# Last ConvFFN of a hybrid backbone: down projection with tokens on partitions, accumulated in four PSUM banks while the features come

## The chip, the cores and the metric

One Trainium2 chip (trn2); the kernel runs on 1 core. The metric is device time in microseconds (us), of one launch. Engines: PE (matrix products; PEld is its loading of stationary operands), DVE, ACT, POOL, and SP, which issues most transfers.

## The reference

The trunk has two layers (DEPTH 2), on 256 context and 256 latent tokens of 1024 features. After the mixing sub-layer each layer has a ConvFFN; the last one runs on the latent tokens alone, and the result is normalised:

```python
def conv_ffn(h, w_up, cw, cb, w_down):
    u = depthwise_conv(h @ w_up, cw, cb, FFN_CONV // 2)
    up, gate = jnp.split(u, 2, axis=-1)
    return (jax.nn.gelu(gate) * up) @ w_down
...
        x = x + mx[5] * conv_ffn(modulate(rms_norm(x, norm_ffn[l]), mx[3], mx[4]),
                                 w_up[l], ffn_conv_w[l], ffn_conv_b[l], w_down[l])
...
    return rms_norm(x, final_norm)
```

`w_up` is 1024 x 5632, `w_down` 2816 x 1024, `mx[5]` a gate per feature, `rms_norm` divides a token by the root of its mean square over the 1024 features and multiplies by a gain per feature. All in float32.

## The kernel before

Activations are kept with features on partitions: `xr[j]` (j = 0 to 7) holds 128 features of all 512 tokens. Each float32 operand of a large product is split into two float32r tiles, high and low (`split`, L155: ACT casts the high part, L151; DVE subtracts for the low one, L158), and `gemm` (L137) issues three products per 128 features of the contraction: high x high, high x low, low x high. The helper `mm` records them all at L129.

Weights come in chunks of up to 1 MB (`chunk`, L161; three slots `raw`, issued by SP in program order), and are split in units of up to 128x1024 into three slots `wh` and three `wl` (`unit`, L192). A slot is free again when PE has done the products of the unit in it.

`ffn` (L1101) works on 22 tiles of 128 gated features, in pairs. For a pair it projects two `up` and two `gate` tiles (`project`, tile `proj`, 24 products of 256 columns each in the last layer), and for each `conv` (L1112) empties the PSUM bank in three passes: ACT's scaled copy (L1114) and two DVE passes for the neighbouring tokens (L1116, L1119). Then gelu (ACT, L1180), the product with `up` (POOL, L1181), and the split into the pair `gTh`, `gTl`. The projections rotate through five PSUM banks `mm`.

`down(k0, k1)` runs twice. After 16 feature tiles it takes the first 14: for each of 8 tiles of 128 output features `m`, the products with `w_down` (stationary) over 14 feature tiles (moving, 256 tokens) into one bank `down`, which DVE then adds into `xr[m]` with the gate (`residual`, L1066). After the last feature it takes the other 8 feature tiles, again for 8 tiles `m` (`finish`, L1077, tile `out`). There, behind each `m`, stand the addition into `xr[m]` (L1070), the square for the norm (ACT, L440, summed by POOL, L442), and `to_tokens` (L1194): DVE multiplies by the final gain (`yf`, L1198), PE transposes two blocks of 128x128 (`yt`, L1201), DVE and ACT copy them into the rows `y`. After the last one come the sums of squares over partitions (products with ones, tile `ss`), root, reciprocal, a scaling of four half rows `y` of 128x512 (L1295 on ACT, L1297 on DVE) and four stores (L1298).

At the start of the stage stand the sums of squares of the mixing sub-layer's result (`ss`), `1/rms` spread over the partitions by PE (`nb`), and `modulate` (L471) for 8 tiles: DVE `hf`, ACT `hh`, DVE `hl`. The first two `up` tiles are projected together, as the tiles `hh`, `hl` come.

The instructions are recorded in program order and a scheduler places them on each engine's queue, which then runs strictly in that order; `prio(150)` lets it take a part 150 instructions earlier.

```python
                    if together - 1 <= m < HELD[l]:
                        finish(
                            held, gT[k0:k1], [Y], gate, t0, squares, to_tokens if last else None,
                            cut=k1 - k0 - 2 if len(held) > 1 else 0,
                        )
```

Of the kernel before, what the change touches and what calls it, by code (L numbers as in the profile page):

```python
# [69 lines left out]
def backbone(ctx: ExitStack, tc: tile.TileContext, a: dict, out: bass.AP):  # L70
# [33 lines left out]
    def banks(alias={}, **tags):  # L104
        """A pool of PSUM banks under the given tags for a part of the program."""
# [12 lines left out]
    def prio(n):  # L118
        """The scheduler takes this part of the program so many instructions earlier."""
# [11 lines left out]
    def keep_busy(n, tag):  # L131
        """Products that nothing reads, to keep the array's clock up through a wait."""
# [11 lines left out]
    def warm(func):  # L144
        """Has the tables of func loaded ahead of its first use."""
# [9 lines left out]
    def split(hi, lo, src, lo_eng=None, hi_eng=None):  # L155
        """src = hi + lo exactly, each in float32r"""
# [41 lines left out]
    def columns(w, c0, c1):  # L198
        """Units of 128 columns of the weight matrix w (K <= 1024 rows), in order."""
# [7 lines left out]
    def run(main, side=None, every=1):  # L207
        """Emits a step of side, then so many steps of main, and so on to the end of both."""
# [58 lines left out]
    def params(l, eng, tag="raw", w=2048):  # L267
# [47 lines left out]
        # the queries come scaled for the softmax  # L315
# [3 lines left out]
        # softplus(-lam) = max(-lam, 0) + log1p(exp(-|lam|)), the second as 2 atanh(e / (2 + e))  # L319
# [53 lines left out]
    def ada_quarter(l, blk, part, col, res, tag):  # L373
        """A quarter of each of the two chunks."""
# [21 lines left out]
    def spread(steps, rate):  # L396
        """Emits rate of steps with each load of weights."""
# [15 lines left out]
    def gains(scale, g, fs=(slice(0, 8),), t=None):  # L413
        """norm gain times (1 + scale), per stream"""
# [8 lines left out]
    class SumSquares:  # L423
        """Sums squares of tiles of features, for n tokens, as the tiles come; the last ones stay apart
        and may come in ranges of tokens."""
# [4 lines left out]
        def add(self, i, t, eng=nc.gpsimd, r=None):  # L430
            """tile i"""
# [12 lines left out]
        def inv_rms(self, width, r=None, ps=None):  # L444
            """Token-major for tokens r: token r.start + 128 t + p at [p, t]."""
# [25 lines left out]
    def modulate(j, h, r, rb, gain, shift):  # L471
        """x / rms * gain + shift for tile j and the tokens r of a stream"""
# [9 lines left out]
    def modulated(hs, squares, t0, scale, col, shift, norm="norm_ffn"):  # L482
        """A function to call as the sums of a stream are there: for the FFN it emits the stream, else both at the last."""
# [32 lines left out]
    def project(u, xs, r, parts=None, tag="mm"):  # L516
        """[P features, tokens r of xs] of one unit of weights, in parts of the tokens"""
# [807 lines left out]
```

## Time and profile before

| | |
|---|---|
| time, median of 3 runs (all) | 1419.99 us (1418.11, 1419.99, 1420.43) |
| profiled execution: span from first to last instruction | 1416.0 us; its own time is not listed apart from these runs |
| mean granted TensorE clock | 0.988 |
| PE busy | 1374.2 us, 97% |
| PEld busy | 1172.5 us, 83% |
| DVE busy | 892.9 us, 63% |
| ACT busy | 668.8 us, 47% |
| POOL busy | 231.9 us, 16% |
| HBM | 193.02 MB read, 137 GB/s over the span |

How to read it: busy times are shares of the whole span, over stages with different limits. Products on PE are pipelined, so the duration of one (0.28 us for 256 columns) is longer than the distance to the next; the price of a product is the time of a gapless run divided by its count. Rows of the chain of waits give such runs. The last ConvFFN runs from about 1206 us to the end.

### The profile page before, as it was taken

The page shows a single profiled execution, that of the slowest core. Times are in us where ns is not written, and L with a number is a line of the kernel's source. Part 1 is how long each engine was busy: PE and PEld are TensorE (multiplying, and loading weights), DVE is VectorE, ACT ScalarE, POOL GpSimd, SP SyncE. Part 2 cuts the span into 40 slices and gives each one's busy share as a digit, 9 for nine tenths or more (in the row PEclk, how much of TensorE's full clock was granted, in tenths as well). Part 3 has the DMA queues.
Part 4 walks back from the last instruction along what each step waited for, and adds up shares of the span by engine and source line. Part 5 has one row for each costly group of instructions (what it writes and reads, how often), then busy time and mean ns, then how long its engine had stood idle before and what let it go on. Part 6 is the DMA issues. An engine that isn't in the chain of part 4 may idle for free.

```text
span 1416.0 us, 20938 instructions
## 1 busy us (share of the span) xinstructions
PE 1374.2 (97%) x8362; PEld 1172.5 (83%) x8362; DVE 892.9 (63%) x1451; ACT 668.8 (47%) x1136; POOL 231.9 (16%) x223
## 2 busy tenths in 40 slices
PE   7999999999999999999999999999999999999997
PEld 5676598888888898888888887878688899999997
DVE  3687648667634565555443543687788986777575
ACT  5575635423532444344322433475355665566454
POOL 2021013113200101211100111010122431122012
PEclk9999999999999999999999999999999999999999
DMA  9433715233233502222343337225465666455643
GB/s 332 135 107 131 272 35 170 80 97 100 79 100 110 172 31 90 86 96 87 89 123 120 104 116 245 62 80 191 152 219 183 197 190 199 135 194 175 196 140 100
DMA packets 187777, 195.41 MB, mean 138 GB/s; under 512 B 9340, under 2 KB 178290, under 8 KB 182560
## 3 DMA queue, kind: packets, MB, share of 16 engines
q1 hardware_dynamic: 186624, 193.23, 42.6%
q8 instruction: 65, 1.06, 0.3%
q0 software_dynamic: 1056, 0.86, 0.2%
q14 instruction: 32, 0.26, 0.1%
HBM read 193.02 MB, written 1.05 MB: 137 GB/s over the span
## 4 chain that ended last, share of the span: by engine, by line
PE 85%; DVE 7%; DMA 3%; ACT 2%; issue 2%; SPq 0%; POOL 0%; ACTq 0%; DVEq 0%; POOLq 0%
PE proj L129 49%; PE down L129 8%; PE out L129 7%; PE lat L129 4%; PE pa L129 3%; PE uf L129 2%; PE sc L129 2%; PE pv L129 2%; PE gt L129 2%; DVE wl L158 2%; PE pt L832 1%; DVE wh L153 1%; DMA raw<-in_w_in_dram 1%; DMA raw<-in_w_ada_dram 1%; PE kn L129 1%
## 5 line engine op out<-in xcount | busy, mean ns | idle before, releaser
L158 DVE TENSOR_TENSOR wl<-raw,wh 128x1024 fp32r<-128x1024 f32 (+9 forms) x339 | 339.4, 1014 | 160.8 <-ACT wh L151 156.1
L129 PE MATMUL proj<-hh,wh 128*128 128x512 f32 (+1 forms) x1232 | 417.8, 340 | 5.5 <-DVE sg L989 2.2
L129 PE MATMUL proj<-hh,wl 128*128 128x512 f32 (+1 forms) x1232 | 416.9, 339 | 0.2 <-DVE wl L158 0.2
L129 PE MATMUL proj<-hl,wh 128*128 128x512 f32 (+1 forms) x1232 | 416.8, 339 | 0.0
L151 ACT CAST wh<-raw 128x1024 fp32r<-128x1024 f32 (+7 forms) x275 | 216.3, 808 | 264.0 <-PE proj L129 153.9
L129 PEld LDWEIGHTS proj<-hh,wh 128*128 128x128 f32 x1232 | 236.1, 192 | 31.9 <-issue 3.1
L129 PEld LDWEIGHTS proj<-hh,wl 128*128 128x128 f32 x1232 | 236.1, 192 | 25.3 <-DVE wl L158 0.7
L129 PEld LDWEIGHTS proj<-hl,wh 128*128 128x128 f32 x1232 | 236.0, 192 | 24.5
L1181 POOL TENSOR_TENSOR gate<-gate,up 128x512 f32<-128x512 f32 (+1 forms) x44 | 55.3, 1257 | 445.4 <-ACT gate L1180 424.7
L153 DVE CAST wh<-raw 128x1024 fp32r<-128x1024 f32 x64 | 54.4, 853 | 52.7 <-PE proj L129 46.4
L129 PE MATMUL down<-gTh,wh 128*128 128x512 f32 (+1 forms) x224 | 75.5, 337 | 0.0
L129 PE MATMUL down<-gTh,wl 128*128 128x512 f32 (+1 forms) x224 | 75.4, 337 | 0.0
L129 PE MATMUL down<-gTl,wh 128*128 128x512 f32 (+1 forms) x224 | 75.3, 336 | 0.0
L158 DVE TENSOR_TENSOR gTl<-gate,gTh 128x512 fp32r<-128x512 f32 (+1 forms) x44 | 24.6, 559 | 78.5 <-ACT gTh L151 78.5
L129 PE MATMUL pa<-raw,cvec 128*32 128x512 f32 (+1 forms) x576 | 62.7, 457 | 3.9 <-DMA raw<-in_w_ada_dram 3.8
L442 POOL TENSOR_TENSOR sq<-sq,sq 128x256 f32<-128x256 f32 (+1 forms) x28 | 31.6, 1129 | 198.6 <-ACT sq L440 197.0
L1070 DVE SCALAR_TENSOR_TENSOR xr<-out,ada,xr 128x256 f32<-128x256 f32 x48 | 22.2, 480 | 44.1 <-PE out L129 44.1
L129 PE MATMUL out<-mh,wl 128*128 128x256 f32 (+1 forms) x152 | 47.4, 312 | 0.0
L129 PE MATMUL out<-mh,wh 128*128 128x256 f32 (+1 forms) x152 | 47.4, 313 | 0.0
L129 PE MATMUL out<-ml,wh 128*128 128x256 f32 (+1 forms) x152 | 47.4, 312 | 0.0
L151 ACT CAST gTh<-gate 128x512 fp32r<-128x512 f32 (+1 forms) x44 | 22.6, 514 | 51.3 <-POOL gate L1181 51.3
L129 PEld LDWEIGHTS down<-gTh,wh 128*128 128x128 f32 x224 | 42.5, 190 | 4.4
(287 smaller groups left out, 2725.3 us busy)
## 6 DMA issues: line engine op xcount, KB each, us to landing
raw<-in_w_up_dram SPq DMA_DIRECT2D x44, 1024.0 KB, 5.0
raw<-in_w_ada_dram SPq DMA_DIRECT2D x40, 1024.0 KB, 4.9
raw<-in_w_in_dram SPq DMA_DIRECT2D x30, 1024.0 KB, 5.3
raw<-in_w_down_dram SPq DMA_DIRECT2D x16, 896.0 KB, 5.2
raw<-in_w_ada_dram SPq DMA_DIRECT2D x32, 256.0 KB, 7.5
raw<-in_w_in_dram SPq DMA_DIRECT2D x16, 512.0 KB, 4.9
raw<-in_w_out_dram SPq DMA_DIRECT2D x8, 1024.0 KB, 5.3
raw<-in_w_down_dram SPq DMA_DIRECT2D x16, 512.0 KB, 3.8
```

What stands on the lines that cost most here:

```text
L129: pinned(nc.tensor.matmul(o, lhsT, rhs, start=start, stop=stop))
L151: nc.scalar.copy(out, in_)
L153: eng.tensor_copy(out, in_)
L158: (lo_eng or nc.vector).tensor_tensor(lo, src, hi, op=ALU.subtract)
L442: eng.tensor_tensor(self.terms[0][:, r], self.terms[0][:, r], sq[:, r], op=ALU.add)
L832: nc.tensor.transpose(o[:, c], probs[i][:, kt * P : (kt + 1) * P], ident)
L1070: nc.vector.scalar_tensor_tensor(xr[m][:, r], o[:, y], gate[:, s, m : m + 1], xr[m][:, r], op0=ALU.mult, op1=ALU.add)
L1181: nc.gpsimd.tensor_tensor(g, g, us[z], op=ALU.mult)
```

## The change

The code before the last ConvFFN stays. In the last layer `ffn` takes another path:

- `down` with tokens on partitions: for a feature tile `k`, the features `gT[k]` (128 features x 128 tokens) are the stationary operand and a row block of `w_down` (128 features x 512 output features) the moving one. Four sums (2 token tiles x 2 halves of the output features) stay in four PSUM banks `acc` over all 22 feature tiles. The products of the pair `i - 2` follow the projections of the pair `i`.
- the projections have three banks `mm`; the first two use banks `acc`, which are not needed yet.
- `row_of` spreads the gate of the output features over all partitions (8 products with the identity, two copies by ACT), and the final gain is loaded as such rows by a transfer that POOL issues.
- `token_major` transposes the residual to tokens, in two steps inside the stage (16 blocks of 128x128, four copies of 128x512 by ACT).
- `down_last` takes the last four feature tiles: 18 and 19 for all four banks, then 20 and 21 bank by bank. Behind each bank: times the gate row, plus the residual (DVE, 128x512), square with its sum over the row (ACT), times the gain (POOL, for the last bank DVE). Behind each token tile: root, reciprocal, scaling of two half rows (DVE and ACT), two stores.
- `to_tokens`, `final_gains` and the sums of squares over partitions go.

```diff
-    def finish(held, xs, qs, gate, t0, squares, also=None, then=None, cut=0):
+    def finish(held, xs, qs, gate, t0, squares, then=None, cut=0):
...
+        accs, rows_ = [], {}
+        def row_of(cols):
+            t = slot("row", "row", F32, D)
+            for z in range(2):
+                o = bank("rowb", "mm")
+                for i in range(4):
+                    j = 4 * z + i
+                    mm(o[:, i * P : (i + 1) * P], cols[:, j : j + 1].to_broadcast([P, P]), ident, True, True)
+                nc.scalar.copy(t[:, z * 512 : (z + 1) * 512], o)
+            return t
+        def token_major():
+            rows_["gain"] = slot("row", "row", F32, D)
+            nc.gpsimd.dma_start(rows_["gain"], a["final_norm"].unsqueeze(0).to_broadcast([P, D]))
+            rows_["gate"] = row_of(ada_cols[2][:, 1, 8:16])
+            yield
+            rows_["x"] = [slot("xt", "row", F32, D) for _ in range(2)]
+            for tt in range(2):
+                for z in range(2):
+                    o = bank("xtb", "mm")
+                    for i in range(4):
+                        nc.tensor.transpose(
+                            o[:, i * P : (i + 1) * P], xr[4 * z + i][:, CTX + tt * P : CTX + (tt + 1) * P], ident
+                        )
+                    nc.scalar.copy(rows_["x"][tt][:, z * 512 : (z + 1) * 512], o)
+                yield
+        def down_part(k, w, tt, z):
+            if not accs:
+                accs.extend([bank("acc") for _ in range(2)] for _ in range(2))
+            q, c = slice(tt * P, (tt + 1) * P), slice(z * 512, (z + 1) * 512)
+            gemm(accs[tt][z], [(gT[k][0][:, q], gT[k][1][:, q], w[0][:, c], w[1][:, c])], k == 0, k == NF - 1)
+        def down_tokens(k):
+            ws = down_weights(k)
+            for i in range(2):
+                for tt in range(2):
+                    for z in range(2):
+                        down_part(k + i, ws[i], tt, z)
+        def down_last(k):
+            ws = {}
+            for k2 in range(k, NF, 2):
+                ws[k2], ws[k2 + 1] = down_weights(k2, "wd")
...
+            for tt in range(2):
+                for z in range(2):
+                    for k2 in range(first, NF):
+                        down_part(k2, ws[k2], tt, z)
+                    with prio(150):
+                        c, y = slice(z * 512, (z + 1) * 512), ys[tt][z]
+                        nc.vector.tensor_tensor(y, accs[tt][z], rows_["gate"][:, c], op=ALU.mult)
+                        nc.vector.tensor_tensor(y, y, rows_["x"][tt][:, c], op=ALU.add)
+                        junk = slot("sq", "s", F32)
+                        nc.scalar.activation(junk, y, AF.Square, accum_out=ssq[:, tt, z : z + 1])
+                        e = nc.vector if tt and z else nc.gpsimd
+                        e.tensor_tensor(yg[tt][z], y, rows_["gain"][:, c], op=ALU.mult)
+                with prio(150):
+                    r = small.tile([P, 1], F32, tag="ry", name=nm("ry"), bufs=2)
+                    nc.vector.tensor_tensor(r, ssq[:, tt, 0:1], ssq[:, tt, 1:2], op=ALU.add)
+                    nc.scalar.activation(r, r, AF.Sqrt, bias=eps, scale=1.0 / D)
+                    nc.vector.reciprocal(r, r)
+                    nc.vector.tensor_scalar(yg[tt][0], yg[tt][0], r, None, op0=ALU.mult)
+                    nc.scalar.activation(yg[tt][1], yg[tt][1], AF.Copy, scale=r)
+                    for z in range(2):
+                        nc.sync.dma_start(out[0, tt * P : (tt + 1) * P, z * 512 : (z + 1) * 512], yg[tt][z])
...
+        if last:
+            side = token_major()
+            with phase("ffn", gT=16, c=8, row=4, wd=8, y=8):
+                with banks(acc=4, mm=3):
+                    next(side)
+                    for i in range(0, NF, 2):
+                        pair_of_tiles(i)
+                        if 2 <= i < NF - 2:
+                            down_tokens(i - 2)
+                        if i >= 4:
+                            next(side, None)
+                    down_last(NF - 4)
+            return
...
-    squares = SumSquares(8, T - CTX)
-    ffn(1, columns_of[1], adas[1], True, h_ffn1, ups1, None, squares, None, None)
-    r = squares.inv_rms(D)
...
+    ffn(1, columns_of[1], adas[1], True, h_ffn1, ups1, None, None, None, None)
```

(`pair_of_tiles(i)` is the body of the old loop over pairs; `down_weights(k)` loads and splits the weights of two feature tiles.)

The scheduler's order moves with it at three places. On ACT, at the start of the last ConvFFN, where the features `hh` are made (`wh` is a weight split, `row` the spread gate), before:

```order
L455 ACTIVATE r_11068<-ss_11062,eps 128x2
L476 ACTIVATE hh_11075<-hf_11091,ada_109 128x256
L476 ACTIVATE hh_11077<-hf_11095,ada_109 128x256
L476 ACTIVATE hh_11079<-hf_11099,ada_109 128x256
L476 ACTIVATE hh_11081<-hf_11103,ada_109 128x256
L151 CAST wh_11197<-raw_11195 128x1024
```

and with the change:

```order
L455 ACTIVATE r_11062<-ss_11056,eps 128x2
L476 ACTIVATE hh_11069<-hf_11085,ada_108 128x256
L1167 COPY row_11129<-rowb_11130 128x512
L476 ACTIVATE hh_11071<-hf_11089,ada_108 128x256
L1167 COPY row_11129<-rowb_11136 128x512
L476 ACTIVATE hh_11073<-hf_11093,ada_108 128x256
L476 ACTIVATE hh_11075<-hf_11097,ada_108 128x256
L151 CAST wh_11206<-raw_11204 128x1024
```

The two copies of the gate's row stand between the first, second and third `hh`.

On PE, at the same place (`ss` sums of squares, `nb` the spread of 1/rms, `rowb` the products that spread the gate, `proj` the first two projections), before:

```order
L129 MATMUL ss_11062<-ones,sq_10820 128x2
L129 MATMUL ss_11062<-ones,sq_11054 128x2
L129 MATMUL nb_11063<-ident,r_11068 128x128 x2
L129 MATMUL proj_11133<-hh_11075,wh_11058 128x256
L129 MATMUL proj_11138<-hh_11075,wh_11134 128x256
```

and with the change:

```order
L129 MATMUL ss_11056<-ones,sq_10814 128x2
L129 MATMUL ss_11056<-ones,sq_11048 128x2
L129 MATMUL rowb_11130<-ident,ada_109 128x128
L129 MATMUL nb_11057<-ident,r_11062 128x128 x2
L129 MATMUL rowb_11130<-ident,ada_109 128x128 x3
L129 MATMUL rowb_11136<-ident,ada_109 128x128 x4
L129 MATMUL proj_11142<-hh_11069,wh_11052 128x256
L129 MATMUL proj_11147<-hh_11069,wh_11143 128x256
```

One of the eight row products stands ahead of `nb`, seven between it and the first projection.

On DVE, behind the last products, before (`yt` the transposed blocks, `fn` the gain):

```order
L1070 SCALAR_TENSOR_TENSOR xr_99<-out_13492,ada_110,xr_99 128x256
L1198 TENSOR_SCALAR yf_13520<-xr_99,fn 128x256
L153 COPY y_13272<-yt_13522 128x128
L456 RECIPROCAL r_13534<-r_13534 128x2
L1297 TENSOR_SCALAR y_13271<-y_13271,r_13534 128x512
L1297 TENSOR_SCALAR y_13272<-y_13272,r_13534 128x512
```

and with the change (`acc` the sums, `row_11129` the gate, `row_11127` the gain, `xt` the residual along tokens, `ssq` the sums of squares):

```order
L1227 TENSOR_TENSOR y_13147<-y_13147,xt_11652 128x512
L1226 TENSOR_TENSOR y_13148<-acc_11444,row_11129 128x512
L1234 TENSOR_TENSOR ry_13177<-ssq 128x1
L1227 TENSOR_TENSOR y_13148<-y_13148,xt_11653 128x512
L1236 RECIPROCAL ry_13177<-ry_13177 128x1
L1226 TENSOR_TENSOR y_13149<-acc_11445,row_11129 128x512
L1237 TENSOR_SCALAR y_13150<-y_13150,ry_13177 128x512
L1227 TENSOR_TENSOR y_13149<-y_13149,xt_11653 128x512
L1231 TENSOR_TENSOR y_13153<-y_13149,row_11127 128x512
L1234 TENSOR_TENSOR ry_13207<-ssq 128x1
L1236 RECIPROCAL ry_13207<-ry_13207 128x1
L1237 TENSOR_SCALAR y_13152<-y_13152,ry_13207 128x512
```

The last bank's product with the gate stands behind the first token tile's reciprocal, and the first token tile's scaling ahead of the last addition.

## Rows read from the trace of the kernel before

**Rows 1.** Busy time by stretch: stretch, us, PE, PEld, DVE, ACT, POOL (count), granted clock, DMA.
```profile
1210.00:1211.00 1.00, 0.81 (x4) 0.51 (x3) 0.15 (x1) 0.00 (x0) 0.00 (x0) 0.50 0.79 266
...
1216.00:1218.00 2.00, 2.00 (x19) 2.00 (x18) 1.97 (x4) 0.46 (x2) 0.00 (x0) 1.00 0.00 0
...
1347.00:1381.00 34.00, 34.00 (x285) 34.00 (x285) 24.75 (x38) 19.80 (x32) 5.07 (x4) 1.00 0.48 147
```

**Rows 2.** Chain that ended last, in order of time: start, us, what.
```profile
711.27 54.71 PE down L129 x241
...
1209.62 1.21 PE nb L129 x4
...
1211.92 94.25 PE proj L129 x768
1306.17 40.32 PE down L129 x336
1346.49 34.56 PE proj L129 x288
```

**Rows 3.** Timeline of PE, from the second `down` on: start, us, engine, line, operation.
```profile
1380.89 0.28 PE L129 MATMUL out<-gTh,wh 128*128 128x256 f32 x1
...
1402.49 0.41 PE L1201 MATMUL yt<-ident,yf 128*128 128x128 f32 x2
...
1407.78 0.28 PE L129 MATMUL ss<-ones,sq 128*128 128x2 f32 x2
```

**Rows 4.** Timelines of DVE, ACT and SP behind the last product.
```profile
1407.98 0.48 DVE L1070 SCALAR_TENSOR_TENSOR xr<-out,ada,xr 128x256 f32<-128x256 f32 x1 [1.50 <-PE out L129]
...
1410.51 1.33 ACT L1295 ACTIVATE y<-y,r 128x512 f32<-128x512 f32 x2
...
1411.02 1.83 SPq L1298 DMA_DIRECT2D out_dram<-y  x4
```

**Rows 5.** Timeline of PE in the attention, a group of four transposes.
```profile
946.13 0.60 PE L832 MATMUL pt<-ident,pr 128*128 128x128 f32 x4
946.48 0.48 PE L129 MATMUL uf<-wh,hh 128*128 128x256 f32 x2
```

**Rows 6.** Timelines of ACT and DVE at the start of the last ConvFFN.
```profile
1211.36 1.31 ACT L476 ACTIVATE hh<-hf,ada 128x256 fp32r<-128x256 f32 x3 [2.09 <-DVE hf L475]
...
1217.73 1.27 DVE L477 SCALAR_TENSOR_TENSOR hl<-hf,ada,hh 128x256 fp32r<-128x256 f32 x3
```

**Rows 7.** Timeline of DVE, the last gate tile: its last pass and its split.
```profile
1385.19 0.48 DVE L1119 SCALAR_TENSOR_TENSOR gate<-proj,cols,gate 128x255 f32<-128x255 f32 x1
...
1387.47 0.42 DVE L158 TENSOR_TENSOR gTl<-gate,gTh 128x256 fp32r<-128x256 f32 x1 [1.80 <-ACT gTh L151]
```

**Rows 8.** Groups by form: line, engine, operation, count | busy us, mean ns | idle before.
```profile
L989 DVE TENSOR_TENSOR sg<-proj,sg 128x512 f32<-128x512 f32 x24 | 16.5, 687 | 9.5 <-PE proj L129 9.5
...
L820 DVE TENSOR_SCALAR pr<-pr,rs 128x512 f32<-128x512 f32 x24 | 11.7, 486 | 0.3
...
L247 ACT ACTIVATE sq<-raw 128x512 f32<-128x512 f32 x8 | 4.9, 616 | 4.6 <-DMA raw<-in_ctx_dram 4.6
...
L247 ACT ACTIVATION_READ_ACCUMULATOR sq<-raw 128x1 f32 x8 | 1.5, 187 | 0.0
...
L948 POOL TENSOR_TENSOR a<-av 128x512 f32<-128x512 f32 x16 | 19.9, 1256 | 5.6 <-ACT av L944 5.6
```

**Rows 9.** Timelines of DVE and POOL, where both work and where POOL works alone.
```profile
1395.86 1.23 DVE L158 TENSOR_TENSOR wl<-raw,wh 128x1024 fp32r<-128x1024 f32 x1 [0.34 <-ACT wh L151]
1396.44 1.22 POOL L442 TENSOR_TENSOR sq<-sq,sq 128x256 f32<-128x256 f32 x1 [2.81 <-ACT sq L440]
1397.00 0.82 DVE L1198 TENSOR_SCALAR yf<-xr,fn 128x256 f32<-128x256 f32 x1
...
1398.62 0.34 DVE L1198 TENSOR_SCALAR yf<-xr,fn 128x256 f32<-128x256 f32 x1
...
1402.61 0.74 POOL L442 TENSOR_TENSOR sq<-sq,sq 128x256 f32<-128x256 f32 x1 [1.92 <-ACT sq L440]
```

More of the change, by code (lines that the diff above doesn't have):

```diff
@@ L1011, in project_out @@
             first()
-            finish(held, merged, ranges(t0), gate, t0, squares, None, then)
+            finish(held, merged, ranges(t0), gate, t0, squares, then)
         def out_units():
@@ L1125, in down @@
             held, gate = [], ada_cols[2][:, :, 8:16]
-            together = 3 if last else 2
+            together = 2
             for m in range(8):
@@ L1142, in down @@
                     if together - 1 <= m < HELD[l]:
-                        finish(
-                            held, gT[k0:k1], [Y], gate, t0, squares, to_tokens if last else None,
-                            cut=k1 - k0 - 2 if len(held) > 1 else 0,
-                        )
+                        finish(held, gT[k0:k1], [Y], gate, t0, squares, cut=k1 - k0 - 2 if len(held) > 1 else 0)
                     if m == 7:
@@ L1150, in down @@
                             first()
-                        finish(held, gT[k0:k1], ranges(t0), gate, t0, squares, to_tokens if last else None, then)
+                        finish(held, gT[k0:k1], ranges(t0), gate, t0, squares, then)
                 else:
@@ L1162, in first_pair @@
         def first_pair():
-            two = [(next(ups), bank("proj", "mm")[:, 0:W]) for _ in range(2)]
+            two = [(next(ups), bank("proj", "acc" if last else "mm")[:, 0:W]) for _ in range(2)]
             for q in streams(t0):
@@ L1170, in first_pair, with pair_of_tiles @@
             return [conv(o, z, "up") for z, (u, o) in enumerate(two)]
+        def pair_of_tiles(i):
+            if i == 0:
+                us = first_pair()
+            else:
+                us = [conv(project(next(ups), h, X), i + z, "up") for z in range(2)]
+            for z in range(2):
+                g = conv(project(next(gts), h, X), NF + i + z, "gate")
+                nc.scalar.activation(g, g, AF.Gelu_apprx_tanh)
+                nc.gpsimd.tensor_tensor(g, g, us[z], op=ALU.mult)
+                hi, lo = pair("gT", "gT", W)
+                split(hi, lo, g)
+                gT.append((hi, lo))
+        if last:
[11 more added lines that the diff above has]
+            return
         with phase("ffn", gT=32, c=8), banks(dict(out="mm"), mm=5, rb=2):
             for i in range(0, NF, 2):
-                if i == 0:
-                    us = first_pair()
-                else:
-                    us = [conv(project(next(ups), h, X), i + z, "up") for z in range(2)]
-                for z in range(2):
-                    g = conv(project(next(gts), h, X), NF + i + z, "gate")
-                    nc.scalar.activation(g, g, AF.Gelu_apprx_tanh)
-                    nc.gpsimd.tensor_tensor(g, g, us[z], op=ALU.mult)
-                    hi, lo = pair("gT", "gT", W)
-                    split(hi, lo, g)
-                    gT.append((hi, lo))
+                pair_of_tiles(i)
                 if i == 14:
@@ L1188, in ffn @@
         ticks.clear()
-    fn = const.tile([P, 8], F32, tag="fn", name="fn")
-    ys = []
-    def to_tokens(j):
-        if not ys:
-            ys.extend([slot("y", "h", F32) for _ in range(2)] for _ in range(2))
-        f = slot("yf", "n", F32)
-        nc.vector.tensor_scalar(f[:, 0:SEQ], xr[j][:, CTX:], fn[:, j : j + 1], None, op0=ALU.mult)
-        pt = bank("yt", "rb")
-        for i in range(2):
-            nc.tensor.transpose(pt[:, i * P : (i + 1) * P], f[:, i * P : (i + 1) * P], ident)
-        for i in range(2):
-            c = slice((j % 4) * P, (j % 4 + 1) * P)
-            copy((nc.vector, nc.scalar)[i], ys[i][j // 4][:, c], pt[:, i * P : (i + 1) * P])
     columns_of = [{} for _ in range(DEPTH)]
@@ L1266, in backbone @@
     emit(mix)
[L1268 to L1277 removed]
+    steps = chain(iter([None] * 3), params(1, nc.gpsimd), iter([None] * 2), ada(1, 0))
     h_mix, sq_mix, cs = [], SumSquares(8, T), adas[1]
```

30 lines of the change are left out of this document (12 added, 18 removed).

## The prediction, made before the run

> **What bounds the kernel now.** The page was read first, for its busy times: PE is busy for nearly the whole span, and the other engines far less. That is an average, so the second view was the busy time by stretch, cut at the borders of the last ConvFFN: in 1347 to 1381 PE is busy 34.00 of 34.00 us at the full granted clock, DVE 24.75, ACT 19.80 [rows 1]. The reader is to see there that inside this stage only PE's own time counts. Third came the chain of waits in order of time: from 1211.92 it is the projections, `down` over the first 14 feature tiles, the projections again, all PE without a gap [rows 2]. Fourth, PE's timeline at the end: the first product of the second `down` starts at 1380.89 and the sums of squares come at 1407.78, so 26.89 us hold 192 products and seven of the eight pairs of transposes [rows 3]. Last, what follows: DVE takes the last sum up at 1407.98, ACT scales the last half row until 1411.84, SP issues four stores until 1412.85, and the span ends at 1416.0 [rows 4]. From the last product to the end that is 1416.0 - 1407.78 = 8.2 us, a chain of short steps over DVE, ACT, PE and SP. So a change here is worth what it takes from PE between 1211.92 and 1407.78, plus what it does to the tail.
>
> The sum is made against the profiled execution's span, 1416.0 us. The timed runs have a median of 1419.99 us, 4.0 above it; I hold this difference fixed. What a measurement can tell from no change is 0.2%, 2.8 us.
>
> **The products.** Before, `down` takes 8 output tiles x 22 feature tiles x 3 = 528 products of 256 columns. Now it is 22 x 2 token tiles x 2 halves x 3 = 264 products of 512 columns, with the gated features as the stationary operand. The chain has both sizes in gapless runs: 336 of 256 columns in 40.32 us, 120.0 ns each, and, in layer 0, 241 of 512 columns in 54.71 us, 227.0 ns each [rows 2]. 528 x 0.1200 = 63.36 and 264 x 0.2270 = 59.93 us: **-3.4 us**. Twice 120.0 is 240.0, so a product costs about 13 ns beside its columns, and half of these costs go. The 1056 projections stay as they are.
>
> The Trainium skill states another price (TensorE: Matmul & The Clock Gate, section Back-to-back issue gap): the columns over 2.4 GHz plus 2.5 ns, which is 109 and 216 ns. By that the change would save an estimated 0.7 us here, not 3.4. Both runs of this trace lie 11 ns above the Trainium skill's price, so the sum goes by the runs.
>
> **What stood between the products.** The last 192 products are worth 192 x 0.1200 = 23.04 us of the 26.89, so 3.85 us went to the transposes back to tokens (one pair is in rows 3) and to waits between them. All of it leaves the end: **-3.85 us**. In its place the residual is transposed to tokens inside the stage, 16 transposes in four groups of four. The nearest row is a group of four in the attention, 0.35 us from its start to the next product [rows 5]: 4 x 0.35 = **+1.4 us**, on PE and so on the path. Their four copies out (ACT, 128x512) lie in ACT's idle time, 14 of 34 us [rows 1]; without that cover they would cost some 0.6 us each, as a pass of that size does in the tail below.
>
> **The start.** Eight 128-column products that spread the gate over the partitions now stand on PE around the reciprocal's spread `nb`, and two copies of 128x512 between the first `hh` on ACT. `nb` is two such products (four records) and took 1.21 us at the 0.50 clock [rows 1, 2], so the seven behind it cost up to 4.2 us, or 2.1 at the full clock. PE sat idle there from 1210.83 to 1211.92, so the first projection starts 1 to 3 us later. But it is not PE's start alone that counts: the projections of the first pair follow the features, whose last half is done by DVE at 1219.00 [rows 6]. ACT made the first three `hh` in 1.31 us [rows 6]; now the third waits for the second copy, and that for the last row product, near 1214. DVE can work ahead meanwhile, so the last feature comes some 0.5 to 1.5 us later. Against this, PE now stays busy in the gap. The granted clock was 0.50 (1.2 GHz) in 1210 to 1211 and 1.00 (2.4 GHz) in 1216 to 1218 [rows 1], and the stretch cost 94.25 - 768 x 0.1200 = 2.1 us for it [rows 2]; some may come back. Between -1.5 (most of the 2.1 back) and +2.0 (features late, clock as before) I take **+0.5 us**, nearer to the middle because both act at once.
>
> **What is hidden.** The weight loads and splits keep their amount (22 units of 128x1024 instead of 16 of 896 and 8 of 1024) and are spread over the stage. The scaled additions into the residual inside `down` go; they were off the path. The POOL load of the final gain, 512 KB, has the whole stage. The wait that is added: only three PSUM banks carry projections. A bank is wanted again after two tiles, 2 x 24 x 0.120 = 5.8 us. The slowest emptying that I can see is that of the last gate tile, in a crowded place: its product ended at 1380.89 [rows 3], the second DVE pass at 1385.67 [rows 7], 4.8 us. So it fits, with 1 us to spare. The last features came 1387.89 - 1380.89 = 7.0 us after their product [rows 3, 7]. Now the products of tiles 18 and 19 cover 24 x 0.227 = 5.45 us, tile 20 another 0.7, and ACT's queue there has no weight casts left to put ahead; I take 0, at worst +1.
>
> **The tail.** Times from here count from the last product; its four banks complete at -4.1, -2.7, -1.4 and 0. Per bank DVE multiplies by the gate row and adds the residual, each 128x512, 0.69 us; ACT squares it, 0.62 + 0.19 us for reading the sum; the scaling is 0.49 on DVE [rows 8] and half of 1.33 or more on ACT [rows 4]; POOL multiplies three of the four by the gain, 1.26 us each [rows 8]. Alone, this would follow the banks closely. But POOL and DVE hold each other up: a POOL sum that took 0.74 us took 1.22 while DVE split weights, and ended 0.57 us after the split; the `yf` behind it took 0.82 us instead of 0.34 [rows 9]. So I let DVE's additions and scalings wait for POOL's products: first addition done at -2.5, POOL until -1.25, second addition -0.65, POOL until 0.6, third bank's addition 1.35, POOL until 2.65, scaling of the first row tile 3.0, last addition 3.65, its gain product 4.25, square 4.45, sum, root and reciprocal 5.1, ACT's scaling 5.9, second store issued 6.55. Behind the last issue the span ran on for 1416.0 - 1412.85 = 3.15 us [rows 4]: 9.7 against 8.2, **+1.45 us**. With no hold-ups the same list ends near 8.4, +0.2; with every small operation caught too, some 10.7, +2.5.
>
> **Sum.** -3.4 - 3.85 + 1.4 + 0.5 + 0 + 1.45 = -3.9: span 1412.1, and 1416.1 us as a median.
>
> **Rivals.**
> A. The forecast, 1415.0 to 1417.6 us: 58%.
> B. Nothing catches: DVE and POOL don't meet in the tail (+0.2) and the row products bring the clock back (-1.5 in place of +0.5). -3.9 - 1.25 = -5.2 with the tail alone, -7.2 with both; 1413.8 us lies between. For it: the clock row; against it: the hold-ups in rows 9. 14%.
> C. Start and tail both at their upper ends: -3.9 + 1.5 + 1.05 = -1.35, 1418.6 us, no difference. The features then come late and DVE becomes the bound of the tail. 14%.
> D. The change doesn't give what its counts say: a product's price follows its columns alone, 0.240 us for 512. Then 264 x 0.240 = 63.36 saves nothing, -0.5, 1419.5 us. Against it stand 241 products at 0.227 [rows 2]; only the stationary operand is new. 4%.
> E. Slower: the three banks. ACT takes its queue in order, and a weight cast that waits for PE stands ahead of each tile's first pass. If emptying then takes over 5.8 us, PE waits in every pair of tiles. From 0.7 us per pair on, ten pairs eat the gain and 0.2% more; at 1.0 us it is -3.9 + 10 = +6, 1426 us. Against it: the 4.8 us of rows 7, and the `down` products of 5.4 us per pair, in which banks come free. 10%.
>
> **How the numbers follow.** The range leaves out E and the better half of B: 1413.2 to 1419.4 us. Faster by over 0.2% means below 1417.1: nine tenths of A, all of B, little of C: 0.66. Within: a tenth of A, most of C, D, 0.24. Slower: E, 0.10.
>
> **What would show it.** Products right: runs of `acc` products at 0.227 us start to start; D if 0.240. Transposes: four groups of `xtb` at 0.35. Start: the first `proj` product after 1211.9 and the last `hl` within 1.5 us of 1219.0. Tail: from the last `acc` product to the end 8.4 to 10.7, with additions longer than 0.69 where POOL works. PE idle before `proj` in the stage would mean E. A last gate tile whose `gTl` is later than 6 us after its product would make the prediction wrong at the end of the products.

## The result, and the profile after

| | before | after |
|---|---|---|
| median of 4 runs each | 1419.51 us (1418.11 to 1420.43) | 1411.24 us (1409.83 to 1411.50) |
| profiled execution: own time, span | about 1418, 1416.0 | 1411.2, 1409.3 |
| mean granted clock of that execution | 0.988 | 0.991 |
| PE busy, DVE busy | 1374.2, 892.9 | 1368.5, 889.3 |

The ratio is 0.9945, 95% interval 0.9931 to 0.9959: faster, by some 7.8 us beside these four runs (6.6 beside all runs of the kernel before, see the experiments). The forecast was 1416.1 us, range 1413.2 to 1419.4. The sign was right, and the time lies 2 us under the range.

The changed stage first. Busy time by stretch of the changed kernel; stretch, us, PE, PEld, DVE, ACT, POOL (count), granted clock, DMA, GB/s:

```profile
1206.00:1208.00 2.00, 2.00 (x13) 2.00 (x12) 1.26 (x4) 0.51 (x1) 0.00 (x0) 0.52 1.10 395
1208.00:1210.00 2.00, 2.00 (x13) 2.00 (x13) 1.80 (x5) 1.30 (x3) 0.00 (x0) 0.63 0.13 49
1210.00:1212.00 2.00, 2.00 (x18) 1.91 (x16) 1.29 (x4) 2.00 (x5) 0.00 (x0) 1.00 0.00 0
1240.00:1390.00 150.00, 150.00 (x1075) 141.96 (x1074) 103.33 (x142) 86.80 (x129) 21.34 (x18) 1.00 0.54 176
```

It answers to [rows 1]: PE is busy for all of 1240 to 1390 at the full level of the clock, so three projection banks hold nothing up. The chain of waits of the changed kernel (start, us, what), which answers to [rows 2]:

```profile
1206.70 2.97 PE rowb L129 x14
...
1233.98 5.47 PE acc L129 x24
1239.45 11.51 PE proj L129 x96
...
1388.56 6.84 PE acc L129 x30
```

24 products of 512 columns take 5.47 us, 0.228 each; 96 projections 11.51, 0.120 each. The row products run at about half the clock (0.52 in 1206 to 1208). Timelines of PE, DVE, ACT, POOL and SP of the changed kernel (start, us, engine, line, operation, idle time before), which answer to [rows 4, 5, 7, 9]:

```profile
1256.27 1.03 PE L1181 MATMUL xtb<-ident,xr 128*128 128x128 f32 x8
1257.06 0.36 PE L129 MATMUL proj<-hh,wh 128*128 128x256 f32 x1
...
1392.87 0.43 DVE L158 TENSOR_TENSOR gTl<-gate,gTh 128x256 fp32r<-128x256 f32 x1 [1.80 <-ACT gTh L151]
...
1396.79 0.69 DVE L1226 TENSOR_TENSOR y<-acc,row 128x512 f32<-128x512 f32 x1
1397.51 1.25 DVE L1227 TENSOR_TENSOR y<-y,xt 128x512 f32<-128x512 f32 x1
...
1399.55 0.58 DVE L1234 TENSOR_TENSOR ry<-ssq 128x1 f32<-128x1 f32 x1 [0.19 <-ACT sq L1229]
...
1404.54 0.72 ACT L1238 ACTIVATE y<-y,ry 128x512 f32<-128x512 f32 x1 [0.23 <-DVE ry L1236]
...
1396.92 1.29 POOL L1231 TENSOR_TENSOR y<-y,row 128x512 f32<-128x512 f32 x1 [4.53 <-DVE y L1227]
1398.84 1.28 POOL L1231 TENSOR_TENSOR y<-y,row 128x512 f32<-128x512 f32 x1 [0.63 <-DVE y L1227]
...
1405.50 0.43 SPq L1240 DMA_DIRECT2D out_dram<-y  x1
```

From the first of eight transposes to the next product 0.79 us pass, and the product behind that one comes 0.08 us late: 0.87 us, twice, so 1.74 against the 1.4 of the forecast. The last features are there at 1393.30, 4.9 us after the last projection's place at 1388.4, inside the cover. The last `acc` product starts at 1399.08, so the tail is 10.2 us, against 8.2. The addition at 1397.51 took 1.25 us while POOL multiplied; the single-column sum at 1399.55 took 0.58 us and ended with POOL's second product. The last store was issued by 1405.93, and the span ran on for 3.4 us.

From the root of the last norm ahead of the stage (ACT, L455: 1209.01 before, 1205.21 after) to the end of the span there are 206.99 us before and 204.09 after: **the stage gives 2.9 us. The other 3.8 us of the two spans had been gained before the stage began.** There the two programs' instructions differ in one thing only: the fetch, transpose and copy of the final gains, which rode in layer 0's steps (the gains' step from here on). The chain of the kernel before, at two places where the difference arises:

```profile
892.55 22.14 PE lat L129 x144
...
1072.14 7.50 PE proj L129 x48
```

and of the changed kernel, the same work:

```profile
891.09 21.03 PE lat L129 x144
...
1069.83 6.01 PE proj L129 x48
```

1.1 and 1.5 us. Busy time of PE by stretch around the first place (stretch, us, PE (count), granted clock, DMA, GB/s), in the kernel before:

```profile
888.00:890.00 2.00, 1.14 (x11) 1.00 0.00 0
890.00:892.00 2.00, 1.40 (x9) 0.89 0.00 0
892.00:894.00 2.00, 2.00 (x11) 0.50 0.00 0
894.00:896.00 2.00, 2.00 (x15) 0.76 0.00 0
```

and in the changed kernel:

```profile
888.00:890.00 2.00, 0.92 (x7) 1.00 0.00 0
890.00:892.00 2.00, 1.62 (x13) 1.00 0.00 0
892.00:894.00 2.00, 2.00 (x19) 1.00 0.00 0
```

PE does and waits for the same things, yet the clock goes to 1.2 GHz in one and not in the other. Such a stretch at a granted clock of 0.50 is called a drop below. A third piece is a transfer. PE's timeline of the kernel before, at the adaLN products of layer 1, and the time it waited for their weights:

```profile
868.76 1.06 PE L129 MATMUL pa<-raw,cvec 128*32 128x512 f32 x8 [1.76 <-DMA raw<-in_w_ada_dram]
```

and of the changed kernel, where the longest such wait is a tenth of that:

```profile
871.18 1.06 PE L129 MATMUL pa<-raw,cvec 128*32 128x512 f32 x8 [0.18 <-DMA raw<-in_w_ada_dram]
```

None of these three is tied to the gains' step by itself. e8 below, which is the changed kernel, has a drop at 893 us and waits 1.80 us for the same weights; e4, also the changed kernel, has a drop at 1069. PE by stretch in e8, the same program as in the last rows by stretch:

```profile
894.00:896.00 2.00, 2.00 (x11) 0.50 0.00 0
```

What is tied to the step are two small delays. One is the transpose's own 0.4 us (see e12). The other lies 300 us later, at PE's wait ahead of the drop near 1070; PE's timeline there, in the kernel before and then in the changed kernel:

```profile
1072.14 0.39 PE L129 MATMUL proj<-hh,wh 128*128 128x256 f32 x1 [2.24 <-DVE sg L989]
```

```profile
1069.83 0.38 PE L129 MATMUL proj<-hh,wh 128*128 128x256 f32 x1 [1.89 <-DVE sg L989]
```

In the five profiles of kernels with the step, or with its transpose alone, this wait is 2.24 us (before, e0, e10) or 3.15 us (e2, e12). In the twelve without it is 1.89 or 1.90 us, once 2.08 (e13). Why DVE is 0.35 us later there is open.

### The profile page after: what moved, and what is told of

Same layout as the page of the kernel before. It is cut to its first block, busy times and chain, and to the rows that moved or that the text cites. A ratio compares the mean times of both kernels' runs of the same rounds, so it can differ in the third digit from the quotient of the medians.

```text
span 1409.3 us, 20366 instructions
## 1 busy us (share of the span) xinstructions
PE 1368.5 (97%) x8105; PEld 1156.9 (82%) x8105; DVE 889.3 (63%) x1428; ACT 670.0 (48%) x1133; POOL 229.0 (16%) x220
## 3 DMA queue, kind: packets, MB, share of 16 engines
HBM read 193.54 MB, written 1.05 MB: 138 GB/s over the span
## 4 chain that ended last, share of the span: by engine, by line
PE 86%; DVE 7%; DMA 2%; ACT 2%; issue 2%; SPq 0%; POOL 0%; DVEq 0%; ACTq 0%; POOLq 0%
PE proj L129 49%; PE out L129 7%; PE down L129 5%; PE acc L129 4%; PE lat L129 4%; PE pa L129 3%; PE uf L129 2%; PE sc L129 2%; PE pv L129 2%; PE gt L129 2%; DVE wl L158 2%; PE pt L832 1%; DVE wh L153 1%; DMA raw<-in_w_in_dram 1%; DMA raw<-in_w_ada_dram 1%
## 5 line engine op out<-in xcount | busy, mean ns | idle before, releaser
L442 POOL TENSOR_TENSOR sq<-sq,sq 128x256 f32<-128x256 f32 (+1 forms) x22 | 25.8, 1171 | 183.4 <-ACT sq L440 181.8
L1259 ACT ACTIVATE gate<-gate 128x512 f32<-128x512 f32 (+1 forms) x44 | 23.1, 524 | 46.5 <-DVE gate L1117 46.4
L129 PE MATMUL down<-gTh,wh 128*128 128x512 f32 x112 | 43.8, 391 | 0.0
L129 PE MATMUL down<-gTh,wl 128*128 128x512 f32 x112 | 43.7, 390 | 0.0
L129 PE MATMUL down<-gTl,wh 128*128 128x512 f32 x112 | 43.6, 389 | 0.0
L1070 DVE SCALAR_TENSOR_TENSOR xr<-out,ada,xr 128x256 f32<-128x256 f32 x40 | 18.4, 481 | 38.2 <-PE out L129 38.2
```

What stands on the lines that cost most here:

```text
L129: pinned(nc.tensor.matmul(o, lhsT, rhs, start=start, stop=stop))
L442: eng.tensor_tensor(self.terms[0][:, r], self.terms[0][:, r], sq[:, r], op=ALU.add)
L1070: nc.vector.scalar_tensor_tensor(xr[m][:, r], o[:, y], gate[:, s, m : m + 1], xr[m][:, r], op0=ALU.mult, op1=ALU.add)
L1259: nc.scalar.activation(g, g, AF.Gelu_apprx_tanh)
```

## The experiments

All 15 runs, each beside runs of the kernel before on the same chip. There were four chips: e0 to e3, e4 to e7, e8 to e11 and e12 to e14 ran on one each, where the kernel before had medians of 1417.8, 1417.5, 1417.8 and 1419.0 us. Its 96 runs in all took 1413.6 to 1422.2 us, median 1417.8, mean granted clock 0.9894:

| run | median us (runs) | ratio to before, 95% | mean clock of its runs |
|---|---|---|---|
| e0 before again | 1418.3 (11) | 0.9994 to 1.0012 | 0.9899 |
| e1 before, gains at the program's start | 1417.1 (12) | 0.9985 to 1.0009 | 0.9898 |
| e14 before, gains at the last ConvFFN | 1415.8 (12) | 0.9968 to 0.9989 | 0.9903 |
| e4, e8 the change again | 1410.9 (5), 1411.7 (5) | 0.9944 to 0.9967, 0.9947 to 0.9973 | 0.9924, 0.9922 |
| e9 one copy more | 1411.1 (6) | 0.9947 to 0.9977 | 0.9920 |
| e2, e10 gains' step put back | 1414.8 (12), 1413.8 (11) | 0.9961 to 0.9987, 0.9960 to 0.9983 | 0.9900, 0.9915 |
| e12 its transpose alone | 1413.8 (12) | 0.9961 to 0.9988 | 0.9906 |
| e13 its fetch alone | 1411.4 (6) | 0.9931 to 0.9959 | 0.9915 |
| e3 rows later | 1414.5 (12) | 0.9968 to 0.9987 | 0.9884 |
| e5, e11 tail without POOL | 1411.7 (1), 1409.6 (6) | none, 0.9938 to 0.9972 | 0.9900, 0.9918 |
| e6 rows later, that tail | 1413.9 (10) | 0.9963 to 0.9985 | 0.9889 |
| e7 products halved | 1414.8 (12) | 0.9978 to 0.9999 | 0.9908 |

**Chance or program? e0, e4, e8.** No edit.

> The kernel before, unchanged, run again with a profile and the span and granted clock of every run. Part of the gap between prediction and result lies ahead of the changed stage: the profiled run of the change reaches the last sums of squares of layer 1's mixing (ss) at 1204.3 us, that of the kernel before at 1208.1, and the granted clock dropped to 0.50 near 892 us and 1072 us in the latter alone. Theory A, chance: the drops fall in some executions of either kernel. Then this run's profile lacks at least one of the two drops (ss at 1204 to 1206.5 us, mean clock 0.989 to 0.991), and the time of its runs varies by 2 us and more with the clock. Theory B, the drops belong to this program: ss at 1207.5 to 1208.5, both drops there again, every run 1418 to 1420.5.

> The changed kernel, unchanged, with more runs. With the kernel before run 35 times on this chip (1413.6 to 1422.0, median 1417.8), the four runs of the result (1409.8 to 1411.5 against 1418.1 to 1420.4) may be a lucky sample of one and an unlucky one of the other. Theory A, chance, and the stage's own worth is 2.9 us in the trace: 1413.5 to 1415.5 median with a spread of several us, ratio to the kernel before 0.9965 to 0.9985. Theory B (the missing step of the gains, put back in the run before this, keeps the clock up): 1411 to 1412, ratio 0.995 to 0.9955, the run with the step put back 3 us slower than this one.

> The changed kernel, unchanged, a third time. Nine runs so far took 1409.8 to 1413.7 us, median 1411.2, while kernels whose instructions ahead of the last ConvFFN are the same one by one (rows later, halves, rows later with the new tail) had medians 1.5 to 3 us above what their own stage explains. Theory A, chance of the clock drops in each execution: a median of 1412 to 1415 here, a spread of 4 us or more. Theory P, the low time is a property of this very program: 1410.5 to 1412 again, at most one run in five above 1413.

Both theories held a part. e0's profile has no drop at 1072 (ss at 1207.2) and 41 runs of 96 of the kernel before lie more than 1.5 us from their median: the drops do fall by execution. But the change stayed at 1410.9 and 1411.7, under the forecast of theory A. Over all its 14 runs the change averages 1411.3 us against 1418.0 for 96 of the kernel before: **6.6 us**, at a mean granted clock of 0.9922 against 0.9894. That difference, times the span, is 4 us of full-speed time if every drop hits a busy PE; within the runs of the kernel before alone, the time falls 0.84 us per 0.001 of clock, which makes it 2.4. Over all profiles of the two kernels (before and e0; after, e4 and e8) the mean from the root to the end of the span goes from 207.2 to 203.7 us, and the mean ahead of the root from 1208.5 to 1206.0: **3.5 us in the stage, 2.6 ahead of it.** The clock's share is in both parts.

**The gains' step. e1, e2, e10, e14.** e2 and e10 put it back, e1 and e14 take it out of the kernel before:

```diff
-    steps = chain(iter([None] * 3), params(1, nc.gpsimd), final_gains(), ada(1, 0))
+    steps = chain(iter([None] * 3), params(1, nc.gpsimd), iter([None] * 2), ada(1, 0))
...
+    for _ in final_gains():
+        pass
     squares = SumSquares(8, T - CTX)
```

(This is e14; e1 has one transfer straight into `fn` there, which the scheduler put at the start.)

> The kernel before, with the final gains loaded straight into columns at the start of the program; their fetch, transpose and copy leave the steps that ride in layer 0's last products. The last ConvFFN is the old one. Theory B1, it is this removed step that moved what lies ahead of the changed stage: 3 to 4.5 us faster than before (ratio 0.997 to 0.998), ss near 1204. Theory A (chance) and B2 (it is another part of the program, such as where the tiles lie): within 1 us of the kernel before (ratio 0.9993 to 1.0007).

> The changed kernel with the old fetch, transpose and copy of the final gains put back into layer 0's steps; nothing reads their result. Theory B1: 3 to 4.5 us slower than the changed kernel (about 1415, ratio to the kernel before 0.997), with a drop of the clock near 892 or 1072. Theories A and B2: as the changed kernel, 1410.5 to 1412 (ratio 0.9935 to 0.995).

> The changed kernel with the fetch, transpose and copy of the final gains put back into layer 0's steps, a second time (the first: median 1414.8, 1408.6 to 1418.6). Theories P and B1: 1414 to 1416 again. Theory A: within 1 us of the changed kernel beside it.

> The kernel before with the whole gains' step taken out of layer 0's products and run at the start of the last ConvFFN instead (fetch, transpose and copy among the first projections). Theory B1, the step in layer 0 costs about 3 us wherever the rest of the program stands: 1414 to 1415.5, ratio to the kernel before 0.9975 to 0.9985. Rival, it costs only in the changed program, as the clock drops fall there: within 1.2 us of the kernel before (ratio above 0.999), as with the step at the very start (0.9997).

Put back, it costs 2.1 us beside e8 (e10), and 3.6 us (e2) over the four runs of the result. Moved to the last ConvFFN (e14), it gains the old kernel 3.1 us beside the runs on its chip, 2.0 beside all 96. Moved to the program's start (e1), it gains 0.8, by its interval 2 at most. Three of four speak for theory B1; e1 speaks against its size: 0.8 is about what the two small delays come to (0.75).

**Which part of the step. e12, e13.** Only the transpose of 8 columns with its copy, or only the fetch:

> The changed kernel with the TensorE and VectorE part of the old gains' step put back alone (a transpose of 8 columns of a constant at the same place among layer 0's products, and the copy behind it), no fetch. Whole step back: 1414.8 and 1413.8 in two tries, against 1410.9, 1411.7 and 1411.1 for the changed kernel. If the transpose is what costs: 1413.5 to 1415. If the fetch on GpSimd's queue, or both are needed: 1410.5 to 1412.

> The changed kernel with only the fetch of the final gains put back into layer 0's steps (a transfer of 4 KB issued by GpSimd near 509 us), nothing transposed or copied. If the fetch costs: 1413.5 to 1415. If the transpose does: 1410.5 to 1412.

The loss goes with the transpose and its copy, not with the fetch: 1413.8 against 1411.4, on one chip, and the intervals don't meet. The chain of e12 at that place (start, us, what):

```profile
766.17 10.88 PE proj L129 x48
777.05 0.15 PE pf L1351
777.21 32.89 PE proj L129 x144
```

From the first projection to the end of the 192nd are 43.93 us, against 43.52 in the changed kernel: 0.4 us is its own price. With the 0.35 us at 1070 that is 0.75 us; no row ties the other 1.6 us to it. What the profiles show is that each execution lost the clock four to nine times ahead of its tail, 1.7 us of full-speed work each (the sum of 1 minus the granted clock over the stretches of a drop; a drop of twice the length counts as two). The places are near 20, 70, 512, 890, 926, 1022, 1070 and 1208 us, another selection each time; near 890, 1070 and 1208 the rows show PE waiting ahead of it. Near 1070, where the wait is longer with the transpose, four of the five profiles with it show a drop (e2 and e12 one of twice the length), and five of the twelve without it. That may be where the rest comes from; 17 profiles don't show it.

**Any edit? e9.** One single-column copy on idle POOL behind the last features:

> The changed kernel with one copy of a single column more on GpSimd just behind the last features, where GpSimd is idle; every other instruction is the same. Its own cost: none on the path. Theory A: 1412 to 1415, as the run beside it. Theory P, any change of the program deals the clock drops anew: a median 1.5 to 4 us above the run beside it, or as far below. Theory B1 (only the old gains' step spoils the clock): as the run beside it, 1410.5 to 1412.

As e8. So not every edit deals the drops anew. But e3 and e6 below, which differ from the changed kernel inside the stage alone, have mean clocks of 0.9884 and 0.9889 over their runs and lie 2 to 3 us above what their stages explain. So the gains' step is not the only thing that goes with lost clock, and what decides it is open.

**The start. e3.** `next(side)` ahead of the loop goes; the rows come after the pair with `i` = 4, which is the third (the expectation calls it the fifth):

```diff
-                    next(side)
                     for i in range(0, NF, 2):
...
-                        if i >= 4:
+                        if i >= 4 and i % 4 == 0:
                             next(side, None)
```

> The changed kernel with the gate's and gains' rows (gate copied into token-major rows by 8 products and 2 ScalarE copies, the gains' fetch) made after the fifth pair of features instead of ahead of the first, the transposes of the residual two and four pairs later. Theory S, the rows are what the start costs: the first projection comes 3.8 us after ss instead of 5.0, the last hl ends 10.9 us after ss instead of 11.5, and the 8 products cost 0.9 us in the dense stretch: 0.3 to 1 us faster than the changed kernel. Rival, the start is bounded by the modulation on VectorE and ScalarE anyway: no more than 0.2 us either way from the changed kernel's 1411.2, or slower by the 0.9 us.

Theory S falls: e3 is 3 us slower than the changed kernel. From the root to the last `acc` product it has 194.68 us, against 193.87 with one drop in the stage in both: 0.8 us longer, close to the rival's 0.9. The chain of e3 at the row products:

```profile
1257.53 1.78 PE rowb L129 x16
```

They take 1.78 us in the dense place, and the earlier start gives back about 1 us of it: the first projection comes 2.40 us after the root instead of 4.13. The other 2 us of the 3 lie outside the stage, and the mean clock over its runs is low, 0.9884; why is open. Ahead of the first pair the row products fill PE's wait. Busy time of PE by stretch in e3:

```profile
1206.00:1208.00 2.00, 0.94 (x7) 1.00 0.90 309
1208.00:1210.00 2.00, 0.89 (x6) 1.00 1.02 352
1210.00:1212.00 2.00, 1.87 (x10) 0.56 0.28 109
```

and in e4, the changed kernel, where the stage began with no drop:

```profile
1204.00:1206.00 2.00, 1.29 (x10) 1.00 0.66 163
1206.00:1208.00 2.00, 1.65 (x15) 1.00 1.11 389
1208.00:1210.00 2.00, 2.00 (x18) 1.00 0.61 235
```

In the profiles, kernels without the row products at this start lost 3.4 us of full-speed work there (before, e0, e14, e6: a drop of twice the length) or 1.7 (e1, e3). Kernels with them lost 1.7 (eight profiles) or, in e4, e7 and e10, nothing. One drop of 1.7 there costs the changed kernel 1.15 us: 193.87 against 192.73 from the root to the last `acc` product, in its own three profiles (after and e8 with a drop, e4 without).

**The tail. e5, e11.** POOL's gain products go; three of the four scalings become one DVE operation each, with the gain in it. The scalings and the stores also move behind both token tiles:

```diff
+                nc.vector.scalar_tensor_tensor(
+                    yg[tt][z], ys[tt][z], rs[tt], rows_["gain"][:, c], op0=ALU.mult, op1=ALU.mult
+                )
```

> The changed kernel with its tail rearranged: no product on GpSimd behind the last down products; three of the four scalings are one VectorE operation (y times 1/rms times gain), the fourth a VectorE product under ScalarE's squares and a ScalarE scaling. Read from the trace: from the issue of the last down product to the end of the span. Theory T, GpSimd beside VectorE stretches the path (an addition 1.25 us instead of 0.69, a single-column addition 0.58 instead of 0.16, a scaling 1.05 instead of 0.49): 8.8 to 9.3 us instead of 10.0, every full-width VectorE operation 0.67 to 0.70 us. Rival, the tail is a chain of fixed waits and the stores: 9.7 to 10.3.

> The changed kernel with the tail that leaves GpSimd out, timed (the look before: a tail of 9.28 us from the start of the last down product against 10.22 and 10.18). By its stage 0.9 us faster than the changed kernel beside it. Theories A and P both leave the part ahead of the stage free to differ by 1 to 3 us, which would hide that.

Timeline of DVE, then SP, in e5:

```profile
1398.75 0.69 DVE L1227 TENSOR_TENSOR y<-y,xt 128x512 f32<-128x512 f32 x1
...
1400.72 0.15 DVE L1235 TENSOR_TENSOR ry<-ssq 128x1 f32<-128x1 f32 x1
...
1403.61 2.68 SPq L1250 DMA_DIRECT2D out_dram<-y  x4
```

The addition is back at 0.69, the small sum at 0.15, the tail at 9.28 (e5) and 9.23 us (e11), which is theory T's forecast. The rows show the hold-ups gone; how much of the 0.95 us the new order alone would give was not tried. e11 is the fastest kernel of the study, 1409.6 against 1411.7 beside it; the trace vouches for 0.95 of the 2 us, and the means of the runs lie 1.0 apart.

**Both edits. e6.**

> Both edits, the rows made later and the tail without GpSimd. If each is worth what its own trace shows (0.3 to 1 us at the start, 0.7 to 1.2 at the tail): 1 to 2 us faster than the changed kernel's runs beside it, and its stage from ss to the end of the span 203 to 204 us (205.0 in the changed kernel's profile). Rival: within 0.7 us of the changed kernel's runs.

Neither the expectation nor its rival holds: e6 is 2 to 3 us slower than the changed kernel. The tail's gain stayed (9.24). The rows' loss did too: 195.39 us from the root to the last product, with the longer drop at the start. As e3 it has a low clock.

**A product's price. e7.** Products of 512 columns as two of 256:

```diff
+            n = 256 if 0 < k < NF - 1 else 512
+            for p in range(c.start, c.stop, n):
+                part, o = slice(p, p + n), accs[tt][z][:, p - c.start : p - c.start + n]
```

> The changed kernel with 240 of its 264 down products of 512 columns split into two of 256 columns, over the same tokens and weights. Theory P, a product costs a fixed share beside its columns (0.1200 us for 256, 0.2270 for 512, both from the traces): groups of 24 products take 5.76 us as 48, the stage gets 240 x 0.013 = 3.1 us longer, 3.1 us slower than the changed kernel. Rival D, the price follows the columns alone: 0.1135 us each, no longer than 5.47 us a group, the same time as the changed kernel.

Its chain of waits:

```profile
1238.15 11.52 PE proj L129 x96
1249.67 5.76 PE acc L129 x48
1255.43 0.87 PE xtb L1181 x8
```

5.76 us for 48, 0.1200 each: theory P. From the root to the last product e7 has 195.69 us against the 192.73 of e4, both without a drop, 3.0 more; its median is 3.1 to 4 above that of e8 and e4.

## Why the prediction was right, and where it was wrong

- **Products, -3.4.** 264 x 0.228 = 60.2 us against 63.36: -3.2. Right, and e7 shows that the share beside the columns is what pays. The Trainium skill's price for isolated products (TensorE: Matmul & The Clock Gate, section Back-to-back issue gap), which the prediction set beside its own price, would be 216 ns for 512 columns; the runs here stand at 227 to 228, so the measurement decides.
- **Between the products, -3.85, and transposes, +1.4.** The waits left the end as forecast: the last products run without a gap. The transposes measured 1.74 (2 x 0.87, as in e7's chain), 0.3 more than forecast.
- **The start, +0.5.** Counted from the root, the first projection comes 1.2 us later than before (4.13 against 2.91) and the last feature 0.7 us, both within what the forecast gave them. From the root to the last product the stage went from 198.77 to 193.87, -4.9; less -3.2, -3.85 and +1.74 that leaves +0.4. That it agrees is in part luck, for the remainder hangs on the drops of the two executions. With one drop on either side (e1 198.5, after 193.87) it is +0.7; with none in the changed kernel (e4, 192.73) and the longer one in the kernel before it is -0.7. The forecast had both parts, features late and clock given back, as its ends.
- **Last features, 0; three banks, no wait.** Right: PE has no idle time in 1240 to 1390, so rival E did not come.
- **The tail, +1.45.** Measured +2.0. The hold-ups are there. One was only in the upper end of the forecast, the small operations: the single-column sum took 0.58 us for 0.15. The last issue ended 6.85 us after the last product's start, where the list had 6.55, and the span ran on for 3.4 us behind it instead of 3.15. The multiplications with a bank as one input were not held up: 0.69 us at 1396.79, beside POOL. The Trainium skill (SBUF — State Buffer, section Who interferes with whom) says that a VectorE instruction with two SBUF inputs contends with a GpSimd one that reads SBUF, and that one with at most one SBUF input doesn't, outside the modes in which VectorE uses both of its ports. The trace agrees on the two: 1.25 us for the addition, 0.69 for the multiplication. The scaling of a half row, which has one such input and a column, took 1.05 us beside POOL and 0.49 without (1401.32 and 1404.61); which mode it ran in no run shows.
- **The sum of the stage, -3.9.** Measured -2.9 in these two profiles, and -2.65 between profiles with one drop each at the start (e1 206.74, after 204.09): 1.0 to 1.25 us too much was promised. The largest part of it is the tail's 0.55. Over all profiles of both kernels it is -3.5.
- **What failed: "I hold this difference fixed."** The forecast was a span of 1412.1 us plus 4.0; the profiled execution had 1409.3 plus 1.9. So the time came out 2.1 us under the forecast by the smaller difference between span and time, and 3.8 us under it by what lies ahead of the stage, which this step let stand. The stage itself took 1.0 us more than its sum. That is the 4.9 us between 1416.1 and 1411.2. In every later run the time is 1.7 to 2.1 us above its own span, so 2 us of the 4.0 came from setting one execution's span beside the median of three others: 1419.99 lies 2.2 above that of 96. And the part ahead of the stage did not stand. Of its 3.8 us in the two profiles, 0.75 belong to the transpose of the gains' step, 0.4 at its place and 0.35 near 1070; the prediction gave it no term at all. The wait for weights near 869 is 1.4 and the drops near 891 and 1072 are 1.5 each; against them stand 1.4 us that the changed kernel's execution lost elsewhere, 0.8 of them near 70. These parts change from execution to execution of the same kernel, so the 3.8 hold an amount of luck; over all profiles of the two kernels it is 2.6. That the two kernels differ by 6.6 us in all is measured. That the transpose makes the clock drop more often is what the medians suggest and no row shows; e3 and e6 lost as much without it. It stays open.

## What to carry to other kernels

Before a forecast, set the profiled execution's span beside its own time, and ask how far two executions of the same kernel lie apart; here it was 8.5 us in 1418, more than the change. Cost every instruction that a change removes, also those far upstream of it, and name the places where PE waits briefly: here the clock was lost behind several of them, in some executions. Products put into such a wait cost less than the same products in a dense place (e3: 0.8 us for eight). Keep GpSimd's products away from additions that end the kernel (1.25 us for 0.69).

## What the runs showed of the hardware that was not expected

- The same program at the same place loses the clock in one execution and not in the next (near 892 us: the changed kernel has no drop in its first profile and one in e8, rows above). Over 96 runs of one kernel the mean granted clock went from 0.986 to 0.993, the time from 1422.2 to 1413.6 us. The Trainium skill (TensorE: Matmul & The Clock Gate, section What's actually happening) says that the gate's look at the array runs free of the program, so that the slow products at a kernel's start vary in number from run to run. The runs here agree in that slow stretches vary, and show it in the middle of a kernel; what decides it they don't show.
- Putting back a transpose of 8 columns and its copy, 0.15 us in the chain, went with a median 2.4 us higher. The rows show 0.4 us at its place and 0.35 us at a wait 300 us later; the rest is open.
- Eight products of 128 columns took 1.78 us between gapless products (e3), 0.22 us each. Ahead of the first projections, where PE waits, they cost about 1 us net.
